# Low parts of fp32 weights: subtracted on VectorE and GpSimd, or negated on ScalarE and completed by adding transfers

## Chip, cores and metric

One NeuronCore of one Trainium2 chip runs the whole program. The metric is the device time of one execution in microseconds (us). The kernel before took 2884.54 us (median of 3 runs, 2882.99 to 2892.52).

## What is computed

A four-layer encoder trunk, batch 1, 512 frames plus 16 meta tokens (528 positions), width 1024, all in float32. Layers 0 and 3 mix with a gated DeltaNet, layer 1 with differential attention, layer 2 with a Griffin block (RG-LRU). After each mixer comes a dense squared-ReLU MLP (1024 to 4096 to 1024). Cut to what matters here:

```python
for layer in range(DEPTH):
    u = rmsnorm(h, norm_mix_w[layer])
    y = (gated_deltanet, diff_attention, rglru_block)[layer % 3](u, ...)   # u @ w_in ... @ w_out
    h = h + keep * y
    u = rmsnorm(h, norm_mlp_w[layer])
    h = h + keep * (jnp.square(jax.nn.relu(u @ w1)) @ w2)
h = rmsnorm(h, final_norm_w)
```

Nearly all the work is these products of activations with weights.

## The kernel before

**Products in two parts.** To get float32 accuracy out of the fast fp32r matmul, every operand is cut into a high part (the value rounded to fp32r) and a low part (the value minus the high part). One product is three matmuls into one PSUM tile: high by high, low activation by high weight, high activation by low weight (`part`, `prod_part`, both through line 219). Activations are cut where they are made; weights are cut each time they are used, and that is what the change touches.

**The weights' way.** Weights lie in HBM as 200 rows `wts[r]` of 128 x 2 x 1024 floats, two units to a row. `load` (line 298, SyncE's queue) brings a whole row, 1 MB, into one of two `raw` buffers. `prep` then makes operands from it and `wsplit` cuts each: line 309 is the high part on ScalarE (a cast, out `hi` or `op`), line 310 the low part (a subtraction, out `lo` or `op`) on VectorE or GpSimd. There are two kinds of operand:

- a plain unit, 128 x 1024, of `dn_in`, `da_in`, `lru_in`, `lru_gate`, the `*_out` projections and `w2`. Its parts go to two tiles, `hi` and `lo`. The table `LO_ENG` says who subtracts, by the unit's place in its row ("vg": VectorE for the first, GpSimd for the second); kinds that are not in the table go to GpSimd. So of w2 and the three lru kinds one unit in two is VectorE's.
- w1 is done by a seven-product (Strassen-Winograd) scheme: a row of two units gives seven 128 x 512 operands, A11, A12, S2, A21, A22, S1, A12 (k = 0 to 6), four of them sums made on VectorE (line 332), so three (k = 0, 1, 4) are the weights as they lie in HBM. Both parts share one tile named `op`. GpSimd subtracts for k = 3, VectorE for the other six.

**What sets the order.** All weight tiles come from one ring of seven (`wp`), so a tile is written again once TensorE has done with the operand seven tiles earlier. `unit` keeps operands worth six such tiles prepared ahead. The framework then schedules each engine's instruction stream with its own model of time, so the order on an engine differs from the order of the code; an engine takes its instructions strictly in that order.

```python
self.wp = pool("wp", bufs=7)
...
while sum(q[1] for q in self.wq) < 6 and self.wnext < len(self.items):
    self.prep()
```

**What reads the results.** A PSUM tile (`c`, five of them, or `d`, three) is emptied by VectorE: line 646 for the projections into the mixers (times the norm's factor, out `s`), 597 for w2 into `h`, 616 for the output projections, 546 for the sums of the w1 scheme. The MLP of a layer runs in four groups; a group is four w1 rows (28 products), then eight w2 units (four rows). GpSimd also runs small transfers of the mixers (lines 788, 848, 858, 1098) and some elementwise work.

Of the kernel before, what the change touches and what calls it, by code (L numbers as in the profile page):

```python
# [9 lines left out]
F32 = mybir.dt.float32  # L10
F32R = mybir.dt.float32r
AF = mybir.ActivationFunctionType
ALU = mybir.AluOpType
# [29 lines left out]

LATS = [1.7] * 8 + [1.1]
CORE_DMA = "gggsss"

LO_ENG = {"w2": "vg", "lru_in": "vg", "lru_out": "vg", "lru_gate": "vg"}

PRODS = (11, 21, 2, 3, 4, 1, 22)
OUT_PARTS = {"dn_out": (4, 4), "da_out": (4, 4), "lru_out": (8,)}  # L50
# [97 lines left out]
class K:  # L148
# [148 lines left out]
        m = len(self.rows[r])  # L297
        self.nc.sync.dma_start(raw[:, :m], self.wts[r, :, :m, :])

    def wsplit(self, src, lo_eng, names):  # L300

        nc = self.nc
        n = src.shape[1]
        if n == 512:
            t = self.wp.tile([128, 1024], F32R, tag="w", name=names)
            hi, lo = t[:, :512], t[:, 512:]
        else:
            hi, lo = (self.wp.tile([128, 1024], F32R, tag="w", name=f"{k}{names}") for k in ("hi", "lo"))
        nc.scalar.copy(hi, src)  # L309
        lo_eng.tensor_tensor(lo, src, hi.bitcast(F32), ALU.subtract)  # L310
        return hi, lo

    def prep(self):

        if self.wnext >= len(self.items):
            return
        nc = self.nc
        r, k = self.items[self.wnext]
        self.wnext += 1
        self.load(r)  # L320
        raw = self.raws[r]
        unit = self.rows[r][0]
        if unit[0] != "w1":
            key = self.rows[r][k]
            eng = nc.vector if r < 2 or LO_ENG.get(key[0], "gg")[k] == "v" else nc.gpsimd
            self.wq.append((key, 2) + self.wsplit(raw[:, k], eng, f"{r}_{k}"))
        else:
            A11, A12, A21, A22 = raw[:, 0, :512], raw[:, 0, 512:], raw[:, 1, :512], raw[:, 1, 512:]
            if k == 0:
                self.s12 = [self.L1(self.getl()), self.L1(self.getl())]  # L330
            S1, S2 = self.s12
            add = lambda o, a, b, op: self.sadd(k).tensor_tensor(o, a, b, op)  # L332
            if k == 2:
                add(S1, A21, A22, ALU.add)
                add(S2, S1, A11, ALU.subtract)
            elif k == 3:
                add(A21, A11, A21, ALU.subtract)
            elif k == 6:
                add(A12, A12, S2, ALU.subtract)
            src = (A11, A12, S2, A21, A22, S1, A12)[k]  # L340
            eng = nc.vector if k != 3 else nc.gpsimd
            self.wq.append((unit + (k,), 1) + self.wsplit(src, eng, f"op{r}_{k}"))
        if k == 0:
            self.load(r + 1)

# [1014 lines left out]
```

## Time and profile before

The profiled execution took 2883.85 us, of which the core's instructions span 2882.1 us.

| | us | of the span |
|---|---|---|
| profiled execution | 2883.85 | |
| span, first to last instruction | 2882.1 | 100% |
| TensorE (PE) matmul busy | 2717.7 | 94% |
| VectorE (DVE) busy | 2064.5 | 72% |
| ScalarE (ACT) busy | 1291.2 | 45% |
| GpSimd (POOL) busy | 918.0 | 32% |
| moved by DMA | 241.11 MB | 84 GB/s mean |

Shares of the whole span mix stages with different limits, so the stages have to be read apart. By the first and last use of their weights they lie as follows: DeltaNet projections and cores 30 to 407 us, its output projection to 452, MLP 0 to 814, attention to 1148, MLP 1 to 1510, the RG-LRU block to 1720, MLP 2 to 2077, DeltaNet again to 2513, MLP 3 to 2865. A row of a group reads: line, engine, operation, out<-in, shapes, count | busy us, mean ns of one | idle time of the engine just before them and what ended most of it. "s L646" in a wait is the instruction of line 646 that writes tile s.

### The profile page before, as it was taken

What the parts mean: (1) busy time and instruction counts of PE and PEld (TensorE: products, weight loads), DVE (VectorE), ACT (ScalarE), POOL (GpSimd) and SP (SyncE); (2) the same over time, 40 slices, a digit from 0 to 9 for tenths busy, and PEclk for the clock granted to TensorE, in tenths of its full rate; (3) what the DMA queues carried; (4) which work ended last, traced back from release to release, by engine and by line L of the source; (5) the groups of instructions that cost most, each with busy time, mean ns of one, the idle gap of its engine ahead of it and who ended that gap; (6) DMA issues with size and microseconds to landing.
All of it is one profiled execution on the core that took longest, in us unless ns stands there. A gap on an engine that the chain in (4) does not pass through costs nothing. (4 is left out here: it accounts for less than half of the span.)

```text
span 2882.1 us, 54564 instructions
## 1 busy us (share of the span) xinstructions
PE 2717.7 (94%) x22032; PEld 2627.1 (91%) x22032; DVE 2064.5 (72%) x4424; ACT 1291.2 (45%) x2856; POOL 918.0 (32%) x580
## 2 busy tenths in 40 slices
PE   7899998999999998999999889999998989999998
PEld 7898898999988887999998889999988888899997
DVE  6987749667735557876668987776589685677764
ACT  4454436334534444543354654443444554444433
POOL 4534333121243333211134532211454343422213
PEclk9999899999999999999999999999999899999999
DMA  4322212233331120322332112232223221132322
GB/s 145 90 79 73 58 50 76 90 102 103 103 105 64 56 66 31 103 89 88 103 103 74 68 65 97 95 103 89 89 89 93 64 67 52 52 103 95 110 89 74
DMA packets 74508, 241.11 MB, mean 84 GB/s; under 512 B 42278, under 2 KB 42824, under 8 KB 49040
## 3 DMA queue, kind: packets, MB, share of 16 engines
q1 hardware_dynamic: 68112, 222.46, 23.3%
q0 software_dynamic: 5488, 13.98, 2.0%
q8 instruction: 173, 2.83, 0.4%
q10 hardware_dynamic: 656, 1.18, 0.1%
q14 instruction: 79, 0.65, 0.1%
HBM read 229.23 MB, written 11.01 MB: 83 GB/s over the span
## 5 line engine op out<-in xcount | busy, mean ns | idle before, releaser
L310 POOL TENSOR_TENSOR lo<-raw,hi 128x1024 fp32r<-128x1024 f32 x188 | 460.0, 2447 | 836.2 <-PE d L219 450.1
L219 PE MATMUL c<-s,hi 128*128 128x264 f32 (+1 forms) x2768 | 511.7, 284 | 0.0
L219 PE MATMUL d<-s,hi 128*128 128x264 f32 (+1 forms) x2480 | 475.7, 289 | 36.1 <-DVE s L646 22.7
L309 ACT CAST hi<-raw 128x1024 fp32r<-128x1024 f32 x270 | 282.9, 1050 | 412.4 <-PE d L219 217.6
L219 PE MATMUL d<-uh,hi 128*128 128x264 f32 (+1 forms) x1520 | 453.9, 299 | 11.0 <-DVE s L646 10.9
L219 PE MATMUL d<-ul,hi 128*128 128x264 f32 (+1 forms) x1520 | 449.4, 296 | 0.0
L219 PE MATMUL d<-uh,lo 128*128 128x264 f32 (+1 forms) x1520 | 448.2, 295 | 0.0
L219 PEld LDWEIGHTS d<-s,hi 128*128 128x128 f32 x2480 | 391.9, 191 | 44.1 <-DVE s L646 19.0
L219 PEld LDWEIGHTS c<-s,hi 128*128 128x128 f32 x2768 | 430.1, 189 | 0.0
L219 PE MATMUL c<-s,lo 128*128 128x264 f32 (+1 forms) x1384 | 392.1, 284 | 0.0
L219 PE MATMUL d<-s,lo 128*128 128x264 f32 (+1 forms) x1240 | 357.4, 288 | 0.0
L219 PEld LDWEIGHTS d<-uh,hi 128*128 128x128 f32 x1520 | 298.2, 196 | 21.7 <-DVE s L646 14.1
L310 POOL TENSOR_TENSOR op<-raw,op 128x512 fp32r<-128x512 f32 x64 | 114.8, 1793 | 593.0 <-ACT op L309 582.0
L219 PEld LDWEIGHTS d<-uh,lo 128*128 128x128 f32 x1520 | 297.5, 196 | 5.0 <-issue 4.2
L219 PEld LDWEIGHTS d<-ul,hi 128*128 128x128 f32 x1520 | 297.8, 196 | 4.5 <-issue 3.5
L309 ACT CAST op<-raw 128x512 fp32r<-128x512 f32 x320 | 193.2, 619 | 237.2 <-PE c L219 119.4
L219 PEld LDWEIGHTS c<-s,lo 128*128 128x128 f32 x1384 | 261.1, 189 | 0.0
L219 PE MATMUL d<-s,op 128*128 128x264 f32 (+1 forms) x1788 | 242.2, 285 | 8.2 <-ACT s L485 3.8
L219 PEld LDWEIGHTS d<-s,lo 128*128 128x128 f32 x1240 | 237.4, 191 | 1.7 <-issue 1.5
L219 PEld LDWEIGHTS d<-s,op 128*128 128x128 f32 x1788 | 227.7, 190 | 9.7 <-ACT s L485 4.2
L310 DVE TENSOR_TENSOR op<-raw,op 128x512 fp32r<-128x512 f32 x256 | 222.4, 869 | 18.8 <-ACT op L309 18.7
L597 DVE TENSOR_TENSOR h<-h,c 128x264 f32<-128x264 f32 (+1 forms) x169 | 71.8, 425 | 184.2 <-PE c L219 184.0
(269 smaller groups left out, 5734.7 us busy)
## 6 DMA issues: line engine op xcount, KB each, us to landing
raw<-in_wts_dram SPq DMA_DIRECT2D x197, 1024.0 KB
s<-dimg SPq DMA_DIRECT2D x32, 245.0 KB
s<-gd POOLq DMA_DIRECT2D x16, 265.0 KB, 4.5
sa<-s POOLq DMA_DIRECT2D x16, 245.0 KB, 3.2
vs<-vd POOLq DMA_DIRECT2D x1, 2620.0 KB, 19.9
h<-in_hT_dram SPq DMA_DIRECT2D x8, 264.0 KB
s<-vs POOLq DMA_DIRECT2D x8, 264.0 KB, 3.0
raw<-in_wts_dram SPq DMA_DIRECT2D x4, 512.0 KB
```

Source lines behind the costliest of these rows:

```text
L219: return self.nc.tensor.matmul(out, lhsT=lhsT, rhs=rhs, start=start, stop=stop)
L309: nc.scalar.copy(hi, src)
L310: lo_eng.tensor_tensor(lo, src, hi.bitcast(F32), ALU.subtract)
L597: nc.vector.tensor_tensor(h, h, ps, ALU.add)
```

## The change

`wsplit` gets the place in HBM from which the operand was read, where there is one. Then ScalarE, after the high part, also writes minus the high part into the low part's tile, and a GpSimd-issued transfer adds the same weights, read from HBM once more, onto that tile. The plain units of all rows but the first two, and k = 0, 1 and 4 of each w1 row, take this way. The first two rows' units, and k = 2, 3, 5 and 6, are subtracted as before. `LO_ENG` goes. Lines after it move: 298, 309, 310, 332 become 296, 307, 309, 335, and the new instructions are lines 311 (ScalarE) and 312 (transfer).

```diff
-LO_ENG = {"w2": "vg", "lru_in": "vg", "lru_out": "vg", "lru_gate": "vg"}
...
-    def wsplit(self, src, lo_eng, names):
+    def wsplit(self, src, lo_eng, names, dram=None):
...
         nc.scalar.copy(hi, src)
-        lo_eng.tensor_tensor(lo, src, hi.bitcast(F32), ALU.subtract)
+        if dram is None:
+            lo_eng.tensor_tensor(lo, src, hi.bitcast(F32), ALU.subtract)
+        else:
+            nc.scalar.activation(lo, hi.bitcast(F32), AF.Copy, scale=-1.0)
+            nc.gpsimd.dma_start(lo, dram, accum_op=ALU.add)
         return hi, lo
...
             key = self.rows[r][k]
-            eng = nc.vector if r < 2 or LO_ENG.get(key[0], "gg")[k] == "v" else nc.gpsimd
-            self.wq.append((key, 2) + self.wsplit(raw[:, k], eng, f"{r}_{k}"))
+            dram = None if r < 2 else self.wts[r, :, k, :]
+            self.wq.append((key, 2) + self.wsplit(raw[:, k], nc.vector, f"{r}_{k}", dram))
...
             eng = nc.vector if k != 3 else nc.gpsimd
-            self.wq.append((unit + (k,), 1) + self.wsplit(src, eng, f"op{r}_{k}"))
+            dram = {0: self.wts[r, :, 0, :512], 1: self.wts[r, :, 0, 512:], 4: self.wts[r, :, 1, 512:]}.get(k)
+            self.wq.append((unit + (k,), 1) + self.wsplit(src, eng, f"op{r}_{k}", dram))
```

The first place where the order moves is GpSimd in MLP 0, from the last w1 row of its first group, through the group's eight w2 units, into the next group's w1. Before (in a name the first number is the unit's place in its row or k, the last one a serial number):

```order
L310 TENSOR_TENSOR op_3_5894<-raw_5698,op_3_5894 128x512
L310 TENSOR_TENSOR lo_1_6014<-raw_5841,hi_1_6013 128x1024
L310 TENSOR_TENSOR lo_1_6121<-raw_5983,hi_1_6120 128x1024
L310 TENSOR_TENSOR lo_1_6249<-raw_6058,hi_1_6248 128x1024
L310 TENSOR_TENSOR lo_1_6363<-raw_6194,hi_1_6362 128x1024
L310 TENSOR_TENSOR op_3_6486<-raw_6308,op_3_6486 128x512
```

The same place of the same engine in the changed program:

```order
L309 TENSOR_TENSOR op_3_5942<-raw_5742,op_3_5942 128x512
L312 DMA op_4_5960<-in_wts_dram 128x512
L312 DMA lo_0_6029<-in_wts_dram 128x1024
L312 DMA lo_1_6064<-in_wts_dram 128x1024
L312 DMA lo_0_6106<-in_wts_dram 128x1024
L312 DMA lo_1_6173<-in_wts_dram 128x1024
L312 DMA lo_0_6244<-in_wts_dram 128x1024
L312 DMA lo_1_6303<-in_wts_dram 128x1024
L312 DMA lo_0_6360<-in_wts_dram 128x1024
L312 DMA lo_1_6419<-in_wts_dram 128x1024
L312 DMA op_0_6477<-in_wts_dram 128x512
L312 DMA op_1_6483<-in_wts_dram 128x512
```

Four subtractions became eight transfers (the other four were VectorE's), and k = 0, 1 and 4 of w1 came in as transfers; k = 3 stayed.

The second place is ScalarE at the opening of the same w2 units, where the last squared activations (`l`, `s`) are also made. Before:

```order
L309 CAST hi_0_6054<-raw_5983 128x1024
L579 CAST s_5797<-l_5795 128x528
L309 CAST hi_1_6120<-raw_5983 128x1024
L579 CAST s_5940<-l_5938 128x264
L578 ACTIVATE l_5939<-l_5939 128x264
```

In the changed program:

```order
L311 ACTIVATE lo_1_6064<-hi_1_6063 128x1024
L307 CAST hi_0_6105<-raw_6033 128x1024
L582 CAST s_5989<-l_5987 128x264
L581 ACTIVATE l_5988<-l_5988 128x264
L311 ACTIVATE lo_0_6106<-hi_0_6105 128x1024
L581 ACTIVATE l_5988<-l_5988 128x264
L307 CAST hi_1_6172<-raw_6033 128x1024
L582 CAST s_5991<-l_5988 128x264
L581 ACTIVATE l_5987<-l_5987 128x264
L582 CAST s_5991<-l_5988 128x264
L582 CAST s_5989<-l_5987 128x264
L311 ACTIVATE lo_1_6173<-hi_1_6172 128x1024
```

Each cast of a high part is followed, some instructions later, by the negation into the low tile, so squared activations now stand behind negations that wait for TensorE to free a tile.

## Rows read from the trace of the kernel before

**Rows 1.** The page, part 1: engine, busy us (share of the span), instructions.
```profile
span 2882.1 us, 54564 instructions
PE 2717.7 (94%) x22032; PEld 2627.1 (91%) x22032; DVE 2064.5 (72%) x4424; ACT 1291.2 (45%) x2856; POOL 918.0 (32%) x580
```
**Rows 2.** Windows: one w1, one w2 stage, two DeltaNet, attention, RG-LRU.
```profile
core 0: us, PE busy (x) PEld busy (x) DVE busy (x) ACT busy (x) POOL busy (x), PEclk, DMA share, GB/s
551.00:592.00 41.00, 41.00 (x338) 41.00 (x337) 40.04 (x68) 23.22 (x40) 7.96 (x4) 1.00 0.30 103
592.00:639.00 47.00, 47.00 (x389) 47.00 (x388) 23.66 (x41) 12.84 (x21) 8.51 (x4) 1.00 0.27 90
...
1549.00:1720.00 171.00, 140.84 (x1052) 137.99 (x1051) 159.93 (x172) 90.53 (x132) 81.28 (x49) 0.91 0.19 68
30.00:407.00 377.00, 342.94 (x2974) 326.18 (x2973) 284.45 (x813) 175.81 (x562) 156.77 (x112) 0.92 0.25 70
2077.00:2465.00 388.00, 355.37 (x3078) 338.38 (x3077) 285.06 (x817) 177.36 (x565) 160.47 (x115) 0.92 0.26 71
814.00:1148.00 334.00, 319.97 (x2201) 274.91 (x2200) 180.15 (x606) 137.02 (x397) 115.41 (x88) 0.96 0.19 65
```
**Rows 3.** Waits of PE, 1549 to 1720: us in total, times, longest.
```profile
PE d L219 <- DVE s L646: 22.7, 6, 7.1
```
**Rows 4.** Groups of lines 309 and 310, whole span.
```profile
L310 POOL TENSOR_TENSOR lo<-raw,hi 128x1024 fp32r<-128x1024 f32 x188 | 460.0, 2447 | 836.2 <-PE d L219 450.1 <-PE c L219 213.4 <-issue 69.7
L309 ACT CAST hi<-raw 128x1024 fp32r<-128x1024 f32 x270 | 282.9, 1050 | 412.4 <-PE d L219 217.6 <-PE c L219 111.9 <-DMA raw<-in_wts_dram 58.6
L309 ACT CAST op<-raw 128x512 fp32r<-128x512 f32 x320 | 193.2, 619 | 237.2 <-PE c L219 119.4 <-issue 56.9 <-PE d L219 44.0
L310 DVE TENSOR_TENSOR op<-raw,op 128x512 fp32r<-128x512 f32 x256 | 222.4, 869 | 18.8 <-ACT op L309 18.7
L310 DVE TENSOR_TENSOR lo<-raw,hi 128x1024 fp32r<-128x1024 f32 x82 | 119.4, 1457 | 51.1 <-PE c L219 30.6 <-PE d L219 14.7 <-issue 2.3
```
**Rows 5.** Timeline, w1 of MLP 0: start us, us, what; DVE and POOL.
```profile
471.94 0.68 DVE L332 TENSOR_TENSOR raw<-raw,l 128x512 f32<-128x512 f32 x1
482.45 1.29 POOL L310 TENSOR_TENSOR op<-raw,op 128x512 fp32r<-128x512 f32 x1 [10.34 <-ACT op L309]
482.52 1.77 DVE L332 TENSOR_TENSOR raw<-raw,l 128x512 f32<-128x512 f32 x1
```
**Rows 6.** Groups of line 310, 1549 to 1720 us.
```profile
L310 DVE TENSOR_TENSOR lo<-raw,hi 128x1024 fp32r<-128x1024 f32 x10 | 16.9, 1690 | 1.1 <-PE d L219 0.7 <-issue 0.4
L310 POOL TENSOR_TENSOR lo<-raw,hi 128x1024 fp32r<-128x1024 f32 x10 | 26.4, 2641 | 16.9 <-PE d L219 9.2 <-ACT hi L309 7.6
```
**Rows 7.** Timeline, w2 opening: fourth unit's low part, its first use.
```profile
514.92 2.41 POOL L310 TENSOR_TENSOR lo<-raw,hi 128x1024 fp32r<-128x1024 f32 x1 [11.55 <-PE d L219]
...
521.97 0.28 PE L219 MATMUL c<-s,lo 128*128 128x264 f32 x1
```
**Rows 8.** Timeline, steady w1: one operand's high part, its low part's first use.
```profile
553.02 0.62 ACT L309 CAST op<-raw 128x512 fp32r<-128x512 f32 x1
...
561.59 0.40 PE L219 MATMUL d<-uh,op 128*128 128x264 f32 x2
```
**Rows 9.** DMA issues of POOL: count, KB each, median us from issue to landing.
```profile
s<-gd POOLq DMA_DIRECT2D x16, 265.0 KB, 4.5
vs<-vd POOLq DMA_DIRECT2D x1, 2620.0 KB, 19.9
s<-vs POOLq DMA_DIRECT2D x8, 264.0 KB, 3.0
```
**Rows 10.** Line 1098: ns that POOL is held by an issue, min/median/max.
```profile
L1098 POOL DMA_DIRECT2D s<-vs x8: 573/578/671, 847.8 to 1069.1; - x8
```

## The prediction

> **What bounds the kernel now.** I read the page's busy shares first, then the windows by stage, then the waits of TensorE in the stages where it is idle, and last the timelines around single weight tiles. TensorE is busy 94% of the span and VectorE 72% [rows 1], but the stages differ. In an MLP TensorE is busy 41.00 of 41.00 us in the w1 part and 47.00 of 47.00 in the w2 part, at the full granted clock, 1.00, although VectorE is busy 40.04 of the 41 us [rows 2]. No relief of VectorE or GpSimd can shorten these four MLPs, about half the span; they can only be hurt, by a low part that comes late. Elsewhere TensorE has holes: 30.2 us of 171.0 in the RG-LRU stretch, 34.1 and 32.6 in the two DeltaNet stretches, 14.0 in the attention [rows 2]. RG-LRU is VectorE's: it is busy 159.93 of 171 us, and TensorE waits 22.7 us there for the line that empties the PSUM tiles [rows 2, 3]. In DeltaNet VectorE is busy 284.45 of 377 us, so those holes are mostly dependent steps.
>
> **What goes and what comes.** VectorE loses 78 of its 82 subtractions of 128x1024 (four stay in the first two rows) at 1.457 us and 192 of the 256 of 128x512 at 0.869 us: 114 + 167 = 281 us. GpSimd loses 188 at 2.447 us, 460 us [rows 4]. ScalarE gains 266 negations; the nearest row is its own cast of that shape, 1.050 us, and 192 half as long, 0.619 us: 279 + 119 = 398 us, so it goes from 45% to about 59% [rows 1, 4]. GpSimd gains 458 issues, 0.58 us each by the transfer with rows of like form [rows 10], about 265 us. HBM is read for 266 x 0.5 + 192 x 0.25 = 181 MB more.
>
> **Gains.** (a) RG-LRU: ten subtractions of VectorE go, 16.9 us, and ten of GpSimd, 26.4 us [rows 6]. GpSimd's also slow VectorE: the same VectorE addition takes 0.68 us alone and 1.77 us when it meets a GpSimd subtraction that lasts 1.29 us [rows 5]. I count half of each of the ten, 1.2 us, 12 us in all. VectorE falls from 160 to about 131 us, below TensorE's 141 us of work, and the wait moves to TensorE itself. Of the 30 us of holes I take 24: the 22.7 us of evacuation waits and a little more. Bounds: 10, if the evacuations then wait for ScalarE, and 30. (b) DeltaNet: there VectorE had no subtraction of weights, only GpSimd's to stumble over, some 32 in each layer. I take 6 us a layer, 12; bounds 0 and 20 of the 67 us of holes. (c) Attention and the first w1 products of a layer: 4, bounds 0 and 8. Together 40, bounds 10 and 58. Work on a less busy GpSimd and a raw buffer that comes free sooner I cost at nothing: TensorE hides both.
>
> **The cost: when the low part is ready.** The tile of a low part is rewritten as soon as TensorE leaves it. In the tightest steady place, the second unit of the second row of a w2 stage, GpSimd starts at 514.92, released by TensorE, and TensorE's first matmul with that tile starts at 521.97: 7.05 us, of which the subtraction used 2.41 [rows 7]. The changed program keeps this distance, 60 matmuls in TensorE's order. Now the chain is a negation, 1.05 us, then X, issue to landing of a 512 KB adding transfer. It holds TensorE up by 1.05 + X - 7.05, that is from X = 6.0 us on.
>
> No adding transfer is in this trace, so X comes from bounds. Transfers issued by GpSimd land after 3.0 us with 264 KB and 19.9 us with 2620 KB [rows 9], 0.0072 us per KB more. That makes 512 KB 4.8 us if adding is free. Adding must also fetch what lies in the tile; if that counts like a second load, 1024 KB, it is 8.5 us. The row of 265 KB at 4.5 us [rows 9] shows that a neighbour can cost 1.5 us. I take the middle, 6.6 us: 0.6 us late, once in each of 16 MLP groups, 10 us. Bounds: at 4.8 nothing; at 8.5 it is 2.5 us there, and the opening's first low part, 69 matmuls of 0.121 us [rows 2] after its tile is free, 8.35 us, is late by 1.2 as well: 3.7 x 16 = 59 us. All later units of a w2 stage, 100 matmuls apart, have 12 us.
>
> w1 is looser than it looks. An operand's cast starts at 553.02 and TensorE needs the low part at 561.59, 8.57 us [rows 8]; cast and negation take 1.24, and 256 KB lands after at most 4.8 by the same line even counted twice. It would take X of 7.3 us. DeltaNet and attention have at least as much as w2's later units, nearly everywhere.
>
> Behind the waiting instructions: negations wait on ScalarE for TensorE to free a tile, and at the opening of w2 the last squared activations stand behind two or three of them, 3 us. TensorE needs these some 100 matmuls, 12 us, later. On GpSimd, k = 3's subtraction stands ahead of k = 4's transfer, but its tile comes free a product earlier. Both cost nothing by this.
>
> **Sum** against the profiled 2883.85 us: - 40 + 10 = - 30, 2854. The median of the runs shown is 0.7 us above that execution, so 2855.
>
> **Rivals.** **Slower, the added transfer moves twice.** The place is the opening of each w2 stage, the price X; gain and cost cancel at about X = 7.8 us ((7.8 - 6.0) + (7.8 - 7.3) = 2.3 us, 16 times, 37). For it speaks that the engines are not free: their share is 0.30 and 0.27 in an MLP [rows 2] for 8 MB of rows per group, and the change adds 7 MB, so 0.53 if counted once and 0.78 if twice, with loads and additions in each other's way. Against it: 3.0 us for 264 KB. At X = 8.5 the time is 2884 - 40 + 59 = 2903; with the gains at their lower bound 2933; one microsecond of X on top costs 32 more, 2965. The Trainium skill (Collectives: The Full Stack, section "The bandwidth ceiling: the fold count and why AG ≠ RS ≠ AR") says that a reducing transfer reads two sources through one ring and so runs at half the rate of a copy; by that rule X is the upper end and the change loses, and no run here shows it yet. **Much slower, DMA bound.** If an added byte costs three times a plain one, the share in an MLP is 0.285 + 3 x 0.25 = 1.03, the engines are the bound and X is 3.0 + 1272 x 0.0072 = 12.2 us. Then the two places of an opening lose 6.2 and 4.9 us and the five later units about 1.2 each, 17 a group, 275 us: about 3120. **No change.** VectorE's relief is not on the path: RG-LRU's chains go on at the pace of ScalarE, which now has 20 x 1.05 us more in them. Gains at 10, cost 10: 2884. **A larger gain.** The granted clock is 0.91 and 0.92 in RG-LRU and DeltaNet, where TensorE has holes, and 1.00 in the MLPs, where it has none [rows 2]: part of the stretch ran at 1.2 instead of 2.4 GHz. Fewer holes may give some of it back; gains at their bound, 58, and no cost: 2826. That the change doesn't do what it says can be left out: the changed order holds the 266 + 192 negations and as many transfers.
>
> **Chances.** Forecast 0.48, slower by doubling 0.24, DMA bound 0.06, no change 0.15, larger gain 0.07. A measurement of this kernel tells about 0.3%, 8.7 us, from no change. Faster than that: 0.45 of the forecast's 0.48 and the larger gain, 0.52. Slower: the two slow cases and a little of "no change", 0.31. The same: 0.17. The range goes from 2828, nearly the larger gain, to 2965, doubling with small gains and a microsecond of contention; left out are the DMA-bound case and the far end of doubling. The likeliest case alone spans 2835 to 2875.
>
> **What will show it.** The median from issue to landing of the transfers of line 312: under 6 us for 512 KB and TensorE stays at 47.00 of 47.00 in w2; at 8 us the waits of TensorE name a DMA into `lo` at the head of each w2 stage. VectorE at about 130 us of the RG-LRU stretch and its wait on line 646 gone for (a). GpSimd's busy time down by 460 us, ScalarE's up by 398. I am wrong if 256 KB takes over 7.3 us, since then every w1 row is late too, or if ScalarE, at 59%, becomes what RG-LRU and DeltaNet wait for.

## The result and the profile after

The changed kernel takes 2924.44 us (median of 4 runs, 2915.78 to 2933.30), the kernel before on the same chip 2887.62: a ratio of 1.0127, 95% interval 1.0086 to 1.0169. It is slower by some 37 us where 30 us of gain were forecast. The profiled execution took 2915.78 us, 31.9 more than that of before.

The page of the changed kernel, its span, part 1, the two large DMA queues, and the issues (count, KB each, median us from issue to landing):

```profile
span 2914.0 us, 55632 instructions
...
PE 2730.9 (94%) x22032; PEld 2638.1 (91%) x22032; DVE 1649.5 (57%) x4154; ACT 1626.5 (56%) x3314; POOL 831.3 (29%) x850
...
q0 software_dynamic: 71440, 203.80, 39.7%
q1 hardware_dynamic: 68112, 222.46, 22.6%
...
lo<-in_wts_dram POOLq DMA_DIRECT2D x266, 512.0 KB, 7.2
op<-in_wts_dram POOLq DMA_DIRECT2D x192, 256.0 KB, 4.3
```

Against [rows 1], VectorE is 415 us less busy, 134 more than its removed subtractions were worth: what stays on it also runs faster. Two DMA queues carry nearly equal megabytes, q0 (the additions and GpSimd's other transfers) at 39.7% of the engines, q1 (the raw rows) at 22.6%. Windows: MLP 0 of the kernel before; then, of the changed kernel, DeltaNet of layer 0, MLP 0, attention, the two parts of RG-LRU, DeltaNet of layer 3:

```profile
core 0: us, PE busy (x) PEld busy (x) DVE busy (x) ACT busy (x) POOL busy (x), PEclk, DMA share, GB/s
452.00:814.00 362.00, 356.06 (x2896) 355.05 (x2897) 265.44 (x457) 160.47 (x271) 84.06 (x44) 1.00 0.28 95
...
30.00:404.00 374.00, 344.06 (x2974) 326.84 (x2974) 239.50 (x812) 204.70 (x594) 106.86 (x112) 0.92 0.51 115
...
448.00:827.00 379.00, 362.36 (x2896) 359.09 (x2897) 201.41 (x394) 214.54 (x351) 104.05 (x106) 0.98 0.72 171
827.00:1091.00 264.00, 247.12 (x1679) 215.08 (x1678) 100.50 (x441) 119.55 (x320) 50.36 (x68) 0.94 0.48 115
...
1552.00:1688.00 136.00, 124.95 (x984) 122.79 (x982) 112.66 (x149) 94.99 (x135) 60.04 (x53) 0.97 0.66 153
1688.00:1746.00 58.00, 51.65 (x383) 50.62 (x384) 40.01 (x63) 38.36 (x57) 22.62 (x19) 0.92 0.57 126
...
2117.00:2486.00 369.00, 346.59 (x3075) 331.66 (x3074) 235.03 (x817) 208.80 (x598) 109.61 (x114) 0.94 0.55 123
```

The whole MLP had 6 us without a matmul, a granted clock of 1.00 and a DMA share of 0.28 (its steady parts had TensorE full [rows 2]); it now has 17 us without a matmul, a clock of 0.98 and a DMA share of 0.72. Its matmuls are busy 6 us longer as well. Waits of TensorE in the whole changed kernel (total us, times, longest):

```profile
PE c L217 <- DMA lo<-in_wts_dram: 38.3, 24, 3.7
PE d L217 <- DMA lo<-in_wts_dram: 20.6, 7, 6.4
PE d L217 <- DVE s L649: 13.8, 12, 2.9
...
PE d L217 <- DMA op<-in_wts_dram: 4.7, 4, 1.8
...
PE c L217 <- DMA op<-in_wts_dram: 1.0, 2, 0.7
```

58.9 us of waits for low parts of whole units are new (44.5 of them in the four MLPs), and 5.7 for those of w1 operands. What they are at an opening of w2 (MLP 0) stands in the timeline, GpSimd first, then TensorE (start us, us, what, idle before and its end):

```profile
496.81 0.86 POOL L312 DMA_DIRECT2D lo<-in_wts_dram  x1 [6.36 <-ACT l L581]
499.55 0.85 POOL L312 DMA_DIRECT2D lo<-in_wts_dram  x1 [1.88 <-DVE s L583]
502.07 0.86 POOL L312 DMA_DIRECT2D lo<-in_wts_dram  x1 [1.68 <-ACT lo L311]
515.98 0.85 POOL L312 DMA_DIRECT2D lo<-in_wts_dram  x1 [13.04 <-ACT lo L311]
```
```profile
503.06 0.39 PE L217 MATMUL c<-s,lo 128*128 128x264 f32 x1 [1.00 <-DMA lo<-in_wts_dram]
...
509.81 0.39 PE L217 MATMUL c<-s,lo 128*128 128x264 f32 x1 [1.38 <-DMA lo<-in_wts_dram]
...
522.11 0.39 PE L217 MATMUL c<-s,lo 128*128 128x264 f32 x1 [0.37 <-DMA lo<-in_wts_dram]
```

Three additions go out within 5.3 us. The first is used 6.2 us after its issue, the second 10.3 after its own, with 1.00 and 1.38 us of TensorE standing still. The fourth, the place of [rows 7], lands after 6.1 us and costs 0.37.

The additions are not alone on the engines. From the second one's issue to its use, 499.55 to 509.81 us, the two queues have these packets, megabytes and shares:

```profile
q0 software_dynamic: 290, 1.06, 55.1%
q1 hardware_dynamic: 228, 1.74, 47.0%
```

Together that is all the time of the engines, and nearly half of it goes to raw rows that SyncE loads for later units. So the second addition shares the engines with a row as well as with the other additions.

The table below goes through all kernels. For each profiled execution I took the starts of the same-numbered matmuls as stage borders, and the difference of each stage to the same stage before, in us: DeltaNet, attention and RG-LRU with their output projections, and the four MLPs together. The last column is the run's ratio to before with its interval.

| kernel | DeltaNet | MLPs | attention | RG-LRU | median us | ratio, 95% |
|---|---|---|---|---|---|---|
| changed | -23.5 | +58.8 | +11.4 | -15.5 | 2924.4 | 1.0127, 1.0086 to 1.0169 |
| plain copies | -43.4 | -10.2 | +5.3 | -15.5 | 2819.6 | 0.9776, 0.9755 to 0.9798 |
| mixers alone | -21.2 | -0.6 | +14.0 | -15.9 | 2849.1 | 0.9877, 0.9855 to 0.9899 |
| w2 alone | +3.2 | +89.9 | +5.9 | +0.6 | 2980.1 | 1.0323, 1.0297 to 1.0348 |
| w1 alone | -13.0 | -5.8 | -1.5 | +0.1 | 2874.4 | 0.9959, 0.9945 to 0.9974 |
| every second w2 | -27.5 | +1.6 | +10.6 | -16.1 | 2854.2 | 0.9888, 0.9876 to 0.9901 |
| no w2 openings | -19.7 | +10.2 | +13.0 | -16.7 | 2866.9 | 0.9929, 0.9917 to 0.9942 |
| w2 openings only | -32.8 | +30.7 | +12.3 | -15.1 | 2883.3 | 0.9990, 0.9974 to 1.0006 |
| broadcast moved | -29.4 | +72.9 | +8.9 | -15.4 | 2923.2 | 1.0124, 1.0102 to 1.0145 |
| negation moved | -32.5 | +71.1 | +14.6 | -15.5 | 2914.6 | 1.0094, 1.0077 to 1.0111 |
| no w2, no attention | -24.8 | -1.3 | +4.8 | -15.4 | 2844.1 | 0.9848, 0.9835 to 0.9861 |
| half w2, no attention | -21.3 | +0.2 | +5.1 | -15.5 | 2848.4 | 0.9860, 0.9843 to 0.9876 |
| no w2, attention late | -30.0 | -4.3 | +1.2 | -16.2 | 2842.3 | 0.9856, 0.9832 to 0.9880 |

A stage of one execution is not exact. The MLPs of the kernels "broadcast moved" and "negation moved" are the changed kernel's, and stand 12 to 14 us above them (the changed kernel's profiled execution is its fastest); DeltaNet scatters as much, and with it the granted clock: layer 0's stage has 0.92 and 421 us in "no w2, no attention", 0.96 and 408 us in the last kernel. RG-LRU repeats within 2 us.

### The profile page after: what moved, and what is told of

It is laid out like the page before. It is cut to its first block, busy times and chain, and to the rows that moved or that the text cites. A ratio compares the mean times of both kernels' runs of the same rounds, so it can differ in the third digit from the quotient of the medians.

```text
span 2914.0 us, 55632 instructions
## 1 busy us (share of the span) xinstructions
PE 2730.9 (94%) x22032; PEld 2638.1 (91%) x22032; DVE 1649.5 (57%) x4154; ACT 1626.5 (56%) x3314; POOL 831.3 (29%) x850
## 3 DMA queue, kind: packets, MB, share of 16 engines
q0 software_dynamic: 71440, 203.80, 39.7%
q1 hardware_dynamic: 68112, 222.46, 22.6%
## 4 chain that ended last, share of the span: by engine, by line
PE 47%; DVE 8%; DMA 8%; issue 3%; ACT 3%; POOL 1%; DVEq 0%; POOLq 0%; ACTq 0%; SPq 0%
PE d L217 25%; PE c L217 21%; DMA lo<-in_wts_dram 6%; PE c L221 1%; DVE s L1155 1%; DVE l L549 1%; DVE s L642 1%; DMA op<-in_wts_dram 1%; DMA s<-sa 1%; ACT lo L311 0%; DMA s<-gd 0%; DVE l L334 0%; DVE s L649 0%; ACT hi L307 0%; DVE s L1170 0%
## 5 line engine op out<-in xcount | busy, mean ns | idle before, releaser
L311 ACT ACTIVATE lo<-hi 128x1024 fp32r<-128x1024 f32 x266 | 281.6, 1059 | 520.3 <-PE d L217 351.1
L312 POOL DMA_DIRECT2D lo<-in_wts_dram x266 | 232.9, 875 | 1083.6 <-ACT lo L311 924.6
L217 PE MATMUL c<-s,hi 128*128 128x264 f32 (+1 forms) x2768 | 518.4, 287 | 0.0
L217 PE MATMUL d<-s,lo 128*128 128x264 f32 (+1 forms) x1240 | 356.7, 288 | 11.7 <-DMA lo<-in_wts_dram 11.6
L307 ACT CAST hi<-raw 128x1024 fp32r<-128x1024 f32 x270 | 279.8, 1037 | 16.1 <-PE d L217 12.9
L312 POOL DMA_DIRECT2D op<-in_wts_dram x192 | 166.2, 866 | 367.7 <-ACT op L311 285.8
## 6 DMA issues: line engine op xcount, KB each, us to landing
vs<-vd POOLq DMA_DIRECT2D x1, 2620.0 KB, 19.9
```

The source lines that it names most:

```text
L217: return self.nc.tensor.matmul(out, lhsT=lhsT, rhs=rhs, start=start, stop=stop)
L311: nc.scalar.activation(lo, hi.bitcast(F32), AF.Copy, scale=-1.0)
L312: nc.gpsimd.dma_start(lo, dram, accum_op=ALU.add)
```

## Experiments

**1. The price of adding.** The same transfers without the addition, so that a low part's tile ends up with the whole weight.

```diff
-            nc.gpsimd.dma_start(lo, dram, accum_op=ALU.add)
+            nc.gpsimd.dma_start(lo, dram)
```

> The changed kernel with the adding transfers made plain copies: the same 458 transfers, on the same queue, behind the same ScalarE negation, but the weight is copied over the negated high part and not added to it, so a low part in the output's products is the whole weight; nothing else differs. Theory A (the addition takes a DMA engine twice as long per byte, and the queue behind it makes low parts late): packets fall from 328 to about 157 ns, the DMA share of the MLP stages from 0.72 to about 0.4, a 512 KB landing from a median of 7.2 to 4.5 to 5.5 us, the waits for low parts in the MLPs (11 to 12 us each) go, and the run falls from 2924 to 2845 to 2875 us, below the kernel before. Theory B (the route itself, negation, issue on GpSimd and the fixed part of a landing, is what is too long): landings stay above 6.5 us and the run within 10 us of 2924. Theory C (the negation stands too late in ScalarE's queue): landings get shorter, but the waits for low parts stay, and the run stays above 2905.

2819.6 us, even below what theory A gave. The page of this kernel:

```profile
q0 software_dynamic: 71440, 203.80, 26.1%
...
lo<-in_wts_dram POOLq DMA_DIRECT2D x266, 512.0 KB, 4.5
op<-in_wts_dram POOLq DMA_DIRECT2D x192, 256.0 KB, 3.4
```

and its window of MLP 0:

```profile
433.00:792.00 359.00, 356.67 (x2894) 355.18 (x2895) 200.36 (x392) 214.09 (x351) 78.44 (x106) 0.99 0.56 181
```

Same bytes, same packets, same negations, and the MLPs lose nothing. So the fixed part of the route and the negation (theories B and C) are not what w2 pays for; the addition is. Its price: before, q0 had 13.98 MB and 2.0% of the span, 58 us of the engines. Taken off, the 189.8 MB of low parts cost 39.7% of 2914.0 less 58, 1099 us, or 5.8 us per MB by addition; 26.1% of 2819.7 less 58, 678 us, or 3.6 by plain copy; and the raw rows cost 22.6% of 2914.0 for 222.46 MB, 3.0. An added byte costs 1.6 times the same copy and nearly twice a raw byte. The Trainium skill (Collectives: The Full Stack, section "The bandwidth ceiling: the fold count and why AG ≠ RS ≠ AR") says of the reduce of a collective that it reads two sources and so runs at half the rate of a copy. The trace agrees in the direction; against the same copy the factor is 1.6 here and not 2. The DMA share of the MLP fell less than expected, to 0.56 and not 0.4.

The lines of the issues (ns min/median/max that GpSimd is held), first of the changed kernel, then of the plain copies, show that the addition also costs on GpSimd:

```profile
L312 POOL DMA_DIRECT2D lo<-in_wts_dram x266: 837/865/1063, 32.2 to 2881.4; - x133
```
```profile
L312 POOL DMA_DIRECT2D lo<-in_wts_dram x266: 527/530/776, 30.8 to 2784.9; - x133
```

**2. Which weights gain and which lose.** Three kernels keep the additions for one kind each; the others go back to subtraction by the old table. The test stands where `dram` is chosen; `ADDED` is that of the mixers here, ('w2',) in the second kernel and empty in the third, and in the first two w1's `dram` is `None`:

```diff
+ADDED = ('dn_ba', 'dn_in', 'dn_out', 'da_in', 'da_out', 'lru_in', 'lru_gate', 'lru_out')
...
-            dram = None if r < 2 else self.wts[r, :, k, :]
+            dram = None if r < 2 or key[0] not in ADDED else self.wts[r, :, k, :]
```

> The change for the DeltaNet, attention and RG-LRU weights alone; w1 and w2 get their low parts by subtraction as before. Theory A: the MLPs go back to the time before (371, 365, 357 and 352 us or so from their first to their last instruction), the mixers keep what they had in the changed kernel (DeltaNet -28, RG-LRU -17, attention +11 against before): 2887 - 34 = 2853 us, 2840 to 2870. Theory B and C say the same of the MLPs; the rival here is that the mixers' gain was only borrowed from the MLPs behind them (a shorter mixer stage whose first MLP steps wait longer, or a lower granted clock there): then the run comes out at 2875 to 2890.

> The change for w2 alone (128 additions of 512 KB); mixers and w1 as before. Theory A: w2's additions alone still queue three at an opening, but without w1's 192 additions of 256 KB ahead of them and beside them; waits for low parts of 6 to 11 us in each MLP in place of 11 to 12, so the run is 30 to 60 us above the kernel before (2917 to 2947). Rival D (w1's and w2's additions are late only together): w2 alone costs less than 15 us (under 2902).

> The change for three of seven w1 operands alone (192 additions of 256 KB); all other low parts by subtraction as before. Theory A: a 256 KB addition lands in 4.0 to 4.4 us and w1's operands are made two steps ahead, so none is late; w1's steps stay at 41.0 to 41.2 us, and what remains is the relief of VectorE and GpSimd: -6 to +4 us (2881 to 2891). Rival E (w1's additions do harm, because they hold the queue when w2's raw operands are due at the openings): +10 to +30 us.

The mixers alone: 2849, as theory A said (2853); the MLPs are back, nothing was borrowed. w1 alone: 2874, a little better than expected. w2 alone: 2980, 97 us slower and so far worse than theory A's 30 to 60. Windows of MLP 0, w2 alone and then w1 alone:

```profile
450.00:833.00 383.00, 363.77 (x2892) 360.59 (x2893) 230.42 (x440) 188.26 (x303) 72.82 (x60) 0.98 0.51 133
```
```profile
449.00:810.00 361.00, 356.88 (x2894) 355.71 (x2894) 229.17 (x407) 184.97 (x316) 119.11 (x90) 0.99 0.49 129
```

Rival D is out: w2 needs no help from w1 to be late. At a mean DMA share of only 0.51 its additions land after a median of 8.6 us, so it is not the mean share that counts but what meets around one opening. The MLPs lose more than in the changed kernel, though w1's additions are gone: 54.8 us of waits for low parts in place of 44.5. Part is plain: waits of 2.5 us for w1's first subtraction and 1.6 for the norm's factor, which the mixers' and w1's additions had ended, are back in that MLP. The landings are longer too, 8.6 against 7.2 in the median of all weights. At the first opening the first addition is issued at 496.04 us, and TensorE gets it 11.5 us later after a wait of 4.13; meanwhile the queues of this kernel have

```profile
q1 hardware_dynamic: 287, 2.10, 54.6%
q0 software_dynamic: 191, 0.72, 34.7%
```

Raw rows are loaded just then, ahead of the addition and beside it. It is so at the other openings too: over all 16 the first addition lands after a median of 10.1 us, with 6.0 us of the engines' time given to raw rows meanwhile; in the changed kernel it is 5.9 and 2.1 us. No run moved these loads, and what sets their place was not tested. The three differences add up to +97 - 34 - 9 = +53; the change made +37.

**3. Where in w2.** Every second operand back to subtraction; then the two operands with which a group of eight opens; then the complement of the second. Who subtracts is by the old table, as in 2; these lines are left out.

```diff
-            dram = None if r < 2 else self.wts[r, :, k, :]
+            dram = None if r < 2 or (key[0] == "w2" and k == 0) else self.wts[r, :, k, :]
```
```diff
-            dram = None if r < 2 else self.wts[r, :, k, :]
+            dram = None if r < 2 or (key[0] == "w2" and key[2] < 2) else self.wts[r, :, k, :]
```
```diff
-            dram = None if r < 2 else self.wts[r, :, k, :]
+            dram = None if r < 2 or (key[0] == "w2" and key[2] >= 2) else self.wts[r, :, k, :]
```

> The changed kernel, but every second w2 operand (64 of 128, the even output tiles) gets its low part by VectorE's subtraction as before; the other 64 by addition, and all else as in the changed kernel. Theory A: half of w2's additions take half the engine time, and no two of w2's are in flight together, so the MLPs lose at most a quarter of the 17 us that each lost: DMA share of an MLP about 0.5, waits for low parts under 3 us an MLP, run 2855 to 2885 us. Theory A2 (any addition of 512 KB beside the raw loads is too late for w2): each MLP keeps half of its loss, 2885 to 2900.

> The changed kernel, but the first two w2 operands of each group of eight (32 of 128, those that a group opens with) get their low parts by subtraction as before. Theory O (the loss sits at the 16 openings, where three additions are issued within about 5 us; behind them the additions keep pace): the waits for low parts and the low clock behind them go, the MLPs come back to 360 us, run 2855 to 2880. Theory P (w2's additions are late at their steady pace too): the loss falls by a quarter at most, or moves to the third operand: 2900 to 2930.

> The complement of the kernel without additions at the openings: of w2 only the first two operands of each group of eight (32 of 128) by addition, the other 96 by subtraction, all else as in the changed kernel. Theory O (the loss is the opening's first low parts, whatever follows): each of 16 openings still waits 1 to 4 us with a low clock behind it, run 2885 to 2925. Theory O2 (the first low parts are late only because a third addition and the raw load share the engines with them): two additions alone land in 6 to 8 us, run 2850 to 2880. Theory P (a loss at the steady pace): a quarter of 64 us stays, about 2870 to 2880.

Windows of MLP 0, in this order:

```profile
447.00:809.00 362.00, 358.18 (x2896) 357.07 (x2897) 217.10 (x408) 202.04 (x335) 90.06 (x90) 0.99 0.63 156
```
```profile
451.00:816.00 365.00, 358.52 (x2894) 356.65 (x2895) 211.23 (x397) 208.53 (x343) 106.94 (x102) 0.99 0.69 166
```
```profile
442.00:815.00 373.00, 360.58 (x2897) 357.34 (x2898) 217.57 (x404) 193.18 (x327) 113.08 (x94) 0.99 0.55 140
```

Sixty-four additions, never two of w2 in a row, cost the MLPs 1.6 us in all (A holds, A2 is out). Ninety-six that leave out the openings cost 10; thirty-two at the openings alone cost 31. So theory O is right in the main and P wrong: with three quarters of the additions kept, the MLPs lose a sixth, with the opening's quarter alone, half. Their sum is 41 of the 59 us that all 128 cost; stages of one execution scatter by 12 us, so it is not shown that the rest comes only when both are there. The third kernel's run, 2883, fell just outside O's bracket and above the other two: no theory had it. In its first opening the second addition still lands after 8.8 us, so no third one is needed to make it late. Its DMA share, 0.55, is as low as that of the plain copies, which lose nothing: again it is not the mean load alone that decides, but what is in flight together. The first kernel leaves one of the three additions in every opening, so it does not tell whether it helped there or by the wider spacing behind.

**4. Attention.** Its loss was in no term of the forecast. One kernel moves a transfer, `vs<-vd`, to SP's queue; one moves attention's negations to GpSimd; the last adds only behind the stage's start.

```diff
-        nc.gpsimd.dma_start(vs[:, :, :NV], vd[:, None, :].broadcast_to([8, 128, NV]))
+        nc.sync.dma_start(vs[:, :, :NV], vd[:, None, :].broadcast_to([8, 128, NV]))
```

> The changed kernel with one transfer moved: attention's broadcast of 2.62 MB in DRAM (vs<-vd) is issued on SP's queue and not on GpSimd's. Theory Q (attention's 11 us are additions that wait behind this broadcast in GpSimd's queue): the one wait of 6 to 7 us on a low part near the start of attention goes, the longest landing falls from 17 to under 12 us, and the run from 2924 to 2910 to 2918. Theory R (the broadcast fills the DMA engines whatever queue it is on, or it now holds up the raw loads): the wait stays, or is replaced by one on raw operands, and the run stays within 5 us of 2924.

```diff
-            nc.scalar.activation(lo, hi.bitcast(F32), AF.Copy, scale=-1.0)
+            if neg:
+                neg.tensor_scalar(lo, hi.bitcast(F32), -1.0, None, ALU.mult)
+            else:
+                nc.scalar.activation(lo, hi.bitcast(F32), AF.Copy, scale=-1.0)
...
-            self.wq.append((key, 2) + self.wsplit(raw[:, k], nc.vector, f"{r}_{k}", dram))
+            self.wq.append((key, 2) + self.wsplit(raw[:, k], nc.vector, f"{r}_{k}", dram, nc.gpsimd if key[0][:2] == "da" else None))
```

> The changed kernel, but attention's 32 negations run on GpSimd and not on ScalarE; the additions stay. Theory S (what attention loses after its start is ScalarE's: a negation of 1.04 us stands ahead of the softmax exponentials, VectorE waits for them in order, and TensorE for VectorE's evacuations, 1.2 us a head): these waits fall to the 0.5 to 0.7 us of before, the windows behind the stage's first 43 us come back by 5 to 10 us, run 2912 to 2920. Theory T (attention's loss is the additions' lateness alone): no gain, or GpSimd's slower negation makes the additions later, 2922 to 2935.

The changed kernel's start of attention, GpSimd, then TensorE:

```profile
845.00 1.13 POOL L1016 DMA_DIRECT2D vs<-vd  x1 [1.69 <-issue]
848.68 1.20 POOL L447 TENSOR_TENSOR rt<-ms,nhalf 106x5 f32<-106x5 f32 x1 [2.55 <-DVE ms L445]
850.19 0.94 POOL L312 DMA_DIRECT2D lo<-in_wts_dram  x1 [0.31 <-ACT lo L311]
852.57 0.86 POOL L312 DMA_DIRECT2D lo<-in_wts_dram  x1 [1.44 <-ACT lo L311]
```
```profile
867.32 0.59 PE L217 MATMUL d<-uh,lo 128*128 128x264 f32 x1 [6.37 <-DMA lo<-in_wts_dram]
```

The 2.62 MB broadcast takes 19.9 us [rows 9], the two additions behind it 17.1 and 17.2, against 7.2 in the median, and TensorE waits 6.37 us. The plain copies wait there too, 6.5 us once: this wait is the queue's, not the addition's. With the broadcast on SP's queue it is gone; its waits of TensorE from 825 to 870 us:

```profile
PE c L217 <- DVE nm L1066: 4.6, 1, 4.6
PE d L217 <- DMA lo<-in_wts_dram: 3.2, 2, 2.5
```

but 4.6 us for `nm`, the first softmax tile that needs what is broadcast, stand in its place, where before had 2.8 us. So Q had the cause and R the time, 2923 against 2924: TensorE waits for the same broadcast in either case.

With the negations on GpSimd the waits of TensorE on VectorE behind the stage's first 43 us fell from 6.7 us in 6 waits to 4.2 in 5, in S's direction. The median, 2914.6, lies in S's bracket. But the stage did not shorten (+14.6 against +11.4), the profiled execution, 2921.7, is the longest of this kernel's six and above the changed kernel's 2915.8, and the intervals of the two kernels overlap. So the trace doesn't show where the median's 10 us lie, nor the runs that they are a gain. S is not shown.

**5. Putting together.** Three kernels add where it gained. The edit shown is the last one's; its `ADDED` holds all kinds of the mixers, and w1's three additions stay in all three kernels.

> Additions where they gained and subtraction where they lost: DeltaNet, RG-LRU and three of seven w1 operands by addition, w2 and attention by subtraction as before. Theory A: the stages add up, DeltaNet and RG-LRU -20 to -40 together and w1 -9 (its gain in DeltaNet overlaps with theirs): 2830 to 2850 us against 2883 before. Rival: w1's additions load the DMA in the MLPs so that raw w2 operands come late, or DeltaNet's gain was that of w1's alone: 2850 to 2870.

> Additions for DeltaNet, RG-LRU, three of seven w1 operands and every second w2 operand; subtraction as before for attention and for the other half of w2. Theory A: stages add up. The kernel with every second w2 operand took 2854; attention by subtraction gives back 10 to 15 of the 11 to 15 us it lost: 2838 to 2848. Rival: attention's stage gets its loss from its start (the broadcast in the queue, the low clock behind it) and keeps it: 2850 to 2858.

> Additions for DeltaNet, RG-LRU, three of seven w1 operands, and for attention only behind its start (heads 2 to 7 and the output projection); w2 and attention's heads 0 and 1 by subtraction as before. Theory Q (attention loses at its start, where additions wait behind the broadcast): the step of 6 to 11 us within the first 35 us of the stage goes; attention comes out 0 to 8 us above before and its output projection 4 below, run 2836 to 2848, level with the kernel without any addition in attention (2844). Theory S (the loss is spread over the heads): attention stays 12 us or more above before, run 2848 to 2858.

```diff
-            dram = None if r < 2 or key[0] not in ADDED else self.wts[r, :, k, :]
+            dram = None if r < 2 or key[0] not in ADDED or (key[0] == "da_in" and key[2] % 8 < 2) else self.wts[r, :, k, :]
```

2844, 2848 and 2842 us, each about 1.5% faster than before, and none better than the others by more than their intervals. In the last, attention has all its additions but those for heads 0 and 1, and is at +1.2 in place of +11.4. Its waits of TensorE from 800 to 1053 us name no low part:

```profile
PE d L220 <- DVE s L653: 7.6, 7, 1.2
PE c L220 <- DVE nm L1070: 2.7, 1, 2.7
PE c L220 <- POOL rt L451: 0.7, 1, 0.7
```

So Q holds and S falls: the waits that attention lost by sat at its start, in the queue behind one long transfer. They are not the whole of the 11.4 us. By the windows of the stage, TensorE's time without a matmul grew by 7 us, and its matmuls were busy 4 us longer at a granted clock of 0.95 for 0.96; stages without any addition in attention are above before as well (+5.9 with w2 alone, +4.8 and +5.1 in the first two kernels here), with matmuls that are busy 4.5 to 6 us longer at 0.95.

## Why the prediction was wrong

The rival "the added transfer moves twice" is what came, in its place (the openings of w2) and its time, 2903 to 2965 for a measured 2924, though not by one price X; the forecast's sum of - 30 came out at + 37. Step by step:

**Gain (a), RG-LRU, - 24: measured - 15.5.** The evacuation wait of 22.7 us [rows 3] shrank to 3.8, as forecast, and VectorE's busy time in the whole stage fell from 188.8 to 152.7 us. But the holes were not filled by as much. In 194 us of the changed stage TensorE still has 17.4 us without a matmul (136.00 + 58.00 less 124.95 + 51.65), where before had 30.3 in 209.5. The plain copies stop at the same - 15.5, so what is left there is no matter of the addition.

**Gain (b), DeltaNet, - 12: measured - 20 to - 33** in the kernels with additions there. VectorE, with only four weight subtractions there before, falls from 284.45 us [rows 2] to 239.50, and in layer 3 from 285.06 to 235.03: it was slowed by GpSimd's more than I took. TensorE's time without a matmul fell by less, in both layers together from 70 to 55 us in the changed kernel with the output projections, near the 12 that I took. The rest is shorter matmuls at a granted clock that differs between executions, and w1 alone has - 13 without any addition there; so the size of this gain stays uncertain.

**Gain (c), attention and first w1 products, - 4: attention + 11.4.** The additions of its first weights were set against "at least as much" room as w2's, without asking what stands before them in their queue; they landed after 17 us and cost a wait of 6.37. The row was there: `vs<-vd`, 19.9 us [rows 9], used only to price bytes.

**The cost, + 10: measured + 59. This is the step that failed.** It rested on one price X, 6.6 us, at one place a group, the fourth unit. The price for an addition alone was too high, if anything: 5.3 us at least for 512 KB, and 6.1 at the place of [rows 7], which cost 0.37 us where 0.6 was forecast. What failed is that X was taken as one number, for a transfer alone. Three additions in 5 us share the engines with one another, at nearly twice the engine time of a raw byte, and with the raw rows that are loaded in the same microseconds; the second lands after 10.2 us, the third after 11.7. By the prediction's own rule the first low part of an opening should be on time below X = 7.3; with 6.2 it should have been about 1 us early, and was 1.00 us late. Of the 2 us between, 0.97 lie between the end of its cast and the start of its negation, behind two instructions for the squared activations on ScalarE, a queue costed at nothing, as its timeline in the changed kernel shows:

```profile
493.44 1.05 ACT L307 CAST hi<-raw 128x1024 fp32r<-128x1024 f32 x1
494.39 0.63 ACT L582 CAST s<-l 128x528 fp32r<-128x528 f32 x1
494.92 0.65 ACT L581 ACTIVATE l<-l 128x528 f32<-128x528 f32 x1
495.46 1.05 ACT L311 ACTIVATE lo<-hi 128x1024 fp32r<-128x1024 f32 x1
```

The upper bound, 3.7 us a group, 59 in all, has the measured size by luck. It is made of waits alone, from X = 8.5 at two places. Measured over the four MLPs, TensorE's time without a matmul rose by 39 us, from 24.1 to 63.1, and its matmuls were busy 19 us longer, 1447.3 for 1428.1; the granted clock fell from 1.00 to 0.98 in two of the MLPs and from 0.99 to 0.98 in the last. Longer matmuls stood in no term of the sum; how much of the 19 us is the clock's was not separated.

**Smaller terms.** An issue holds GpSimd for 0.87 us, not 0.58: 399 us (232.9 for 266, 166.2 for 192) for a forecast of 265, so GpSimd fell by 87 us in all, where 460 less 265 was forecast. w1 was right: 256 KB lands after 4.3 us, under the 7.3 that was needed, and 5.7 us of waits is all there is. That ScalarE might become the bound did not come; it is busy 56% of the span.

**The chances.** The rival had 0.24, against it "3.0 us for 264 KB". That row is of a lone transfer without addition; here plain copies of 256 KB land after 3.4 us and of 512 KB after 4.5, so it was near the truth for a copy and said nothing of an addition. For the rival spoke the DMA share of 0.78 that it worked out; 0.72 was measured. What else is on the engines in the 7 us in which a transfer must land, here two more additions and a raw row, should have had more weight than the landing of one that is alone.

## What to carry to other kernels

A transfer that must land just in time is costed with those issued within a few microseconds of it, in its queue and on its engines, the loads of other queues among them; a single landing time from a quiet stretch is a lower bound and no more. Adding by DMA pays where the engine that it relieves was waited for and the operand has slack (RG-LRU, DeltaNet, w1), and not in a stage that TensorE already fills, where it can only be late: choose it for each kind of weight. Where a burst was the trouble, replacing every second transfer was enough here.

## What was not expected of the hardware

An addition holds GpSimd longer than the same copy, 865 ns against 530 in the median, at the same bytes and packets. It costs 5.8 us of engine time per MB against 3.6 for a copy on the same queue and 3.0 for the raw rows on the other. And an issue of 128x1024 lands, at its quickest, after 5.3 us by addition and 3.8 by copy; for half the size 4.0 and 3.2, so the second 256 KB cost 1.3 and 0.6.
